# A two-layer hybrid decoder: column group 1 normed for the first tokens inside layer 0's last products, and the parameters loaded behind x's eighth block

## Chip, cores and metric

One core of one Trainium2 chip. The metric is device time in microseconds (us): the median of the runs of a kernel. Before the change three runs took 908.03, 908.29 and 909.82 us, median 908.29 us.

## What is computed

Two decoder layers on x of 256 tokens by 2048 columns (float32). Each layer makes one combined input projection, mixes its columns in three branches (a gated convolution, latent attention, an RWKV-7 scan), makes one output projection and a LayerNorm over each token's row:

```
for l in range(2):
    u = x @ w_in[l]                       # 2048 -> 6016 columns, cut into groups
    y_conv, y_mla, y_rwkv = the three branches of u
    mix = concatenate([y_conv, y_mla, y_rwkv])          # 2048 columns
    x = layer_norm(alpha * x + mix @ w_out[l], ln_g[l], ln_b[l])
```

## The kernel before

**Products in three parts.** Every float32 weight block is split into a rounded half (`hi`, a cast on ACT) and a remainder (`lo`, a subtraction on DVE); x is split in the same way. TensorE (PE) multiplies hi by hi, hi by lo and lo by hi. A weight block lands in one of five raw buffers (pool `wr`), its halves go to one of four pairs of buffers (pool `wh`); SP issues the loads in the order of `plan()`, and the next load waits for a free raw buffer, the next cast for a pair that PE has read to the end.

**Layer 0's start.** The first column group, `k`, needs all of x. `STEPS` (L215) lists the pieces in which x and the weights of `k` arrive together, each one DMA from `xT` (`load_first`, L217): pieces of one or two of the 16 blocks of 128 rows. ACT and DVE split x and the weights of each piece, and PE does 12 matmuls of 256 columns for each block. Behind the last piece (`k0 == 14`) `load_constants` (L164) makes GpSimd (POOL) copy one element of that piece and then issue the loads of `pars` (the per-channel parameters), `cs` (masks and the like), `posi` (positions) and `ones` (a matrix of ones that sums over channels). `load_params` (L248) derives eight small tables `pc` from `pars` on DVE. The group `k` is then mixed with its shifted self into `kx`: four ACT scalings, each with a DVE multiply-add behind it, that read the PSUM accumulator `u_k`. The group `a` follows on PE, in two halves, `u_a_0` and `u_a_1`.

**Accumulators.** Pool `pp` has two buffers of two PSUM banks, for `u_*` and `po_*`, so the third accumulator in a row waits until an earlier one has been read out: `u_a_1` follows `u_k` and `u_a_0`.

**The order of the instructions.** A scheduler orders each engine's instructions by data and buffers. `after(inst, earlier)` adds an order; the list `splits` holds the cast and the subtraction of each weight block in load order, so `after(v, splits[n][1])` places v behind a block's subtraction on DVE.

**From layer 0 to layer 1.** `out_proj` (L1229) makes the output projection in four groups of 512 columns, and group 3 in two halves `i` of 256, for the token halves `h` = 0 and 1. The second half of group 3 is computed for h = 0, then for h = 1. When h = 0 is complete, `root(0)` finds its mean and reciprocal deviation; `row(0)` (matmul `cwt`, cast `ct`) and `norm(0, g)` (a matmul `lw` of 512 columns, and one DVE multiply-add) finish the LayerNorm of column group g. Layer 0 does `norm(0, 0)` between the products of h = 1, at the places `AT[0] = (10, 13)` of 16, and groups 1 to 3 in `rest`, beside layer 1's first products. `add` (L1245) reads an accumulator into the residual `xr`, `keep_warm` issues 12 matmuls `pz` while PE waits for `root(1)`, and `turn` (matmuls `xt`) transposes the normed rows into x of the next layer.

Of the kernel before, what the change touches and what calls it, by code (L numbers as in the profile page):

```python
# [14 lines left out]
ALU = mybir.AluOpType  # L15
# [15 lines left out]
AT = [(10, 13), (4, 8)]  # L31
# [80 lines left out]
def hybrid_layers(ctx: ExitStack, tc: tile.TileContext, x, positions, xT, w_in, w_out, w_uq, w_ukv, par, wa_in, gb_in,  # L112
# [13 lines left out]
    gates, splits = {}, []  # L126
# [40 lines left out]
    def load_constants(x):  # L167

        last = G.tensor_copy(pars[0:1, 0, 0:1], x[0:1, 0:1])
        for to, src in ((pars, par), (cs, cst), (posi, positions[0:1, :].to_broadcast([P, S]))):  # L170
            load = nc.gpsimd.dma_start(to, src)
            after(load, last)
            last = load
        o32 = c4("ones32", (P, 2 * P))
        load = nc.gpsimd.dma_start(o32, sums)
        after(load, last)
        V.tensor_copy(ones, o32)
        loaded.append(load)

    def zeros(rows):  # L180

# [31 lines left out]
    xres = x  # L213
    xs = [pair(f"x0_{g}") for g in range(4)]

    STEPS = [(0, 1), (1, 1), (2, 2), (4, 2), (6, 2), (8, 2), (10, 2), (12, 2), (14, 2)]

    def load_first(k0, n):

        t = s8(f"first{k0}", (P, n, S + 512))  # L220
        in_turn(1, nc.sync.dma_start(t, xT[:, k0:k0 + n, :]))
        with tc.high_priority():
            to, at = xs[k0 // 4], k0 % 4
            split_in(to[:, 0, at:at + n, :], to[:, 1, at:at + n, :], t[:, :, 0:S])
        if k0 == 14:
            load_constants(t[:, 0, :])
        return t[:, :, S:].rearrange("p k (i c) -> p i k c", i=2)

# [19 lines left out]
    def load_params(l):  # L248
        pq = pars[:, l, :]
        pc = cp.tile([P, 29], F32, tag=f"pc{l}", name=f"pc{l}")  # L250
        V.tensor_scalar(pc[:, 0:13], pq[:, Q_MUR:Q_MUR + 13], -1.0, 1.0, ALU.mult, ALU.add)
        V.tensor_scalar(pc[:, 13:21], pq[:, Q_W0:Q_W0 + 8], 0.5, None, ALU.mult)
        V.tensor_scalar(pc[:, 21:25], pq[:, Q_KA:Q_KA + 4], 0.5, None, ALU.mult)
        V.tensor_scalar(pc[:, 25:29], pq[:, Q_KA:Q_KA + 4], -0.5, 1.0, ALU.mult, ALU.add)
        col = lambda j: pq[:, j:j + 1] if j < NQ else pc[:, j - NQ:j - NQ + 1]
        return dict(col=col, om=NQ - Q_MUR, hw=NQ + 13, ha=NQ + 17, hk=NQ + 21, ok=NQ + 25)

# [95 lines left out]
    def acc(name):  # L353

        return pp.tile([P, 2, 512], F32, tag="acc", name=name)
# [857 lines left out]
    def ln_rows(l):  # L1213

        t = sm.tile([P, 2, 16], F32, tag="lnp", name=f"lnp{l}", bufs=1)
        load = nc.gpsimd.dma_start(t, gbp[l])
        after(load, loaded[0])
        hi = sm.tile([P, 2, 16], F32R, tag="lnh", name=f"lnh{l}", bufs=1)
        lo = sm.tile([P, 2, 16], F32R, tag="lnl", name=f"lnl{l}", bufs=1)
        V.tensor_copy(hi, t)  # L1220
        V.tensor_tensor(lo, t, hi.bitcast(F32), ALU.subtract)
        rows = dr.tile([5, D], F32R, tag=f"lnr{l}", name=f"lnr{l}")
        for i, src in enumerate((hi[:, 0], lo[:, 0], hi[:, 0], hi[:, 1], lo[:, 1])):
            nc.gpsimd.dma_start(rows[i].rearrange("(p i) -> p i", p=P), src)
        return rows

    def out_proj(l, ms, xres, last, begin, lnr):
# [86 lines left out]

        def rest(cts):
            for g in range(1, 4):
                for h in range(2):
                    norm(h, g, cts[h])
                yield
                for h in range(2):  # L1320
                    turn(h, g)
# [20 lines left out]
        for g in range(4):  # L1342
            xr = c4(f"xr{l}_{g}", (P, 2, 512))
            after(nc.scalar.dma_start(xr, xres[0, :, g * 512:(g + 1) * 512].rearrange("(h p) c -> p h c", p=P)), begin)
            zs.append(xr)
            gt = s4(f"gb{l}_{g}", (P, 2, 512))
            after(nc.scalar.dma_start(gt, gb_in[l:l + 1, :, g * 512:(g + 1) * 512].to_broadcast([P, 2, 512])), begin)
            gs.append(gt)
            if g < 3:
                pa = acc(f"po{l}_{g}")  # L1350
                po = [pa[:, h, :] for h in range(2)]
                for k0 in ORDER:
                    ws = [weights(f"wo{l}_{g}", k0 + k) for k in (0, 2)]
                    for h in range(2):
                        part(po, h, 512, ws)
                for h in range(2):
                    add(po[h], g, 0, 512, h, g)
                continue
            po, held = [], {}
            for i in range(2):  # L1360
                pa = acc(f"po{l}_{g}_{i}")
                po.append([pa[:, h, 0:256] for h in range(2)])
                held[i] = []
                for k0 in ORDER:
                    held[i].append(weights(f"wo{l}_3_{i}", k0))
                    if not last and i == 0:
                        for h in range(2):
                            part(po[i], h, 256, held[0][-1:])
                if not last and i == 0:
                    for h in range(2):  # L1370
                        add(po[i][h], g, 0, 256, h, 3)
            cts = []

            def turn_row(h):
                ct, m = row(h)
                cts.append(ct)
                return m

            first_rows = {AT[last][0]: lambda: turn_row(0),
                          AT[last][1]: lambda: [norm(0, g_, cts[0])[0] for g_ in range(4 if last else 1)][-1]}  # L1380
            for h in range(2):
                for i in range(2):
                    if not last and i == 0:
                        continue
                    part(po[i], h, 256, held[i], first_rows if h and i else {})
                    add(po[i][h], g, i * 256, 256, h, 3 + i)
                mark.setdefault(l + 1, []).append(root(h))
            if not last:
                xs += [pair(f"x{l + 1}_{g}") for g in range(1, 4)]
            keep_warm()  # L1390
            if last:
                turn_row(1)
                part1(256, 256)
                nc.scalar.dma_start(rows(0)[:, 1], zs[0][:, 1])
                for g_ in range(1, 4):
                    norm(1, g_, cts[1], ((0, 512),) if g_ < 3 else ((0, 256), (256, 256)))
            else:
                turn(1, 0, ((0, 2),))
                t = turn(0, 0, hold=mark[l + 1][1])
                after(part0(256, 256), mark[l + 1][1])  # L1400
                mark[l + 1][1] = t
                part1(256, 256)
                nc.gpsimd.dma_start(rows(0), zs[0])
                turn(1, 0, ((2, 2),))
                turn_row(1)
                run(rest(cts))
                tick()
# [60 lines left out]
```

## Time and profile before

| | |
|---|---|
| median of 3 runs | 908.29 us |
| the profiled execution | 909.28 us |
| its span, first to last instruction | 907.5 us |
| PE busy | 893.1 us (98%) |
| DVE busy | 687.5 us (76%) |
| ACT busy | 486.1 us (54%) |
| GpSimd busy | 24.6 us (3%) |
| mean granted TensorE clock | 0.994 of full speed |
| HBM | 181 GB/s over the span |

A row of a timeline gives start and duration in us, engine, source line, operation, output and inputs, and in brackets how long the engine was idle before and what ended that. Matmuls overlap, so the distance of two starts, not a duration, is what one costs. Nearly all DVE and ACT rows carry L138, a wrapper's line, and are told apart by their tiles.

### The profile page before, as it was taken

The numbers are of one execution on the slowest core, as the hardware profiler recorded it, in microseconds if no ns is written. First come the engines' busy times: TensorE is split into PE (matmuls) and PEld (weight loads), VectorE is DVE, ScalarE is ACT, GpSimd is POOL, SyncE is SP. The second block draws the span as 40 slices with busy tenths as digits, with TensorE's granted clock in tenths as the row PEclk, the third lists the DMA queues.
The fourth block names the chain that finished last, engine by engine and source line by source line (L and its number), as shares of the span: only waits on it lengthen the run. The fifth ranks groups of instructions, "written<-read, shape, count | busy, mean of one in ns | idle before, by whom it ended". The sixth has DMA issues, their size and how long they took to land.

```text
span 907.5 us, 16003 instructions
## 1 busy us (share of the span) xinstructions
PE 893.1 (98%) x6314; PEld 786.7 (87%) x6314; DVE 687.5 (76%) x1166; ACT 486.1 (54%) x752; POOL 24.6 (3%) x47
## 2 busy tenths in 40 slices
PE   8899999999999999999999999999999999999996
PEld 8788888888889888888898888888888998988896
DVE  7677988986558987476775889799765699875665
ACT  6577546444447666544246874564444575765430
POOL 2120000000000000000020000000000000000000
PEclk9989999999999999999999999999999999999999
DMA  9755674666535654696576456646654456547832
GB/s 373 222 139 161 185 208 130 187 197 177 161 111 165 193 161 118 205 325 204 171 225 194 136 190 191 170 124 204 196 173 141 123 158 209 163 118 239 315 119 93
DMA packets 65100, 164.98 MB, mean 182 GB/s; under 512 B 15286, under 2 KB 23782, under 8 KB 65014
## 3 DMA queue, kind: packets, MB, share of 16 engines
q1 hardware_dynamic: 57264, 150.36, 54.4%
q10 hardware_dynamic: 5072, 9.57, 3.0%
q0 software_dynamic: 2688, 4.03, 1.6%
q8 instruction: 49, 0.80, 0.4%
q14 instruction: 27, 0.22, 0.1%
HBM read 158.61 MB, written 5.32 MB: 181 GB/s over the span
## 4 chain that ended last, share of the span: by engine, by line
PE 95%; DVE 2%; ACT 1%; DMA 1%; issue 0%; DVEq 0%; SPq 0%; ACTq 0%
PE po L341 7%; PE u_mg L441 7%; PE po L343 7%; PE po L342 6%; PE u_a L441 4%; PE u_cc L441 3%; PE u_cg L441 3%; PE u_mg L443 3%; PE u_v L441 3%; PE u_cb L441 3%; PE u_ch L441 3%; PE u_cq L441 3%; PE u_rg L441 3%; PE u_r L441 3%; PE u_rg L443 2%; PE u_cg L443 2%
## 5 line engine op out<-in xcount | busy, mean ns | idle before, releaser
L138 DVE TENSOR_TENSOR lo_wo<-w_wo,hi_wo 128x1024 fp32r<-128x1024 f32 x57 | 69.1, 1222 | 45.0 <-ACT hi_wo L138 44.1
L138 ACT CAST hi_wo<-w_wo 128x1024 fp32r<-128x1024 f32 x57 | 59.3, 1050 | 60.1 <-PE po L343 29.9
L441 PE MATMUL u_mg<-x,hi_mg 128*128 128x512 f32 x256 | 90.0, 396 | 0.0
L443 PE MATMUL u_mg<-x,lo_mg 128*128 128x256 f32 x256 | 71.4, 280 | 0.0
L441 PEld LDWEIGHTS u_mg<-x,hi_mg 128*128 128x128 f32 x256 | 47.9, 188 | 10.8
L441 PE MATMUL u_a<-x,hi_a 128*128 128x512 f32 x128 | 48.1, 415 | 3.1 <-DVE u_a L138 3.1
L443 PEld LDWEIGHTS u_mg<-x,lo_mg 128*128 128x128 f32 x256 | 48.3, 189 | 0.2
L341 PE MATMUL po<-hi_wo,ma 128*128 128x512 f32 (+1 forms) x128 | 46.7, 365 | 0.0
L343 PE MATMUL po<-hi_wo,ma 128*128 128x512 f32 (+1 forms) x128 | 46.5, 363 | 0.0
L342 PE MATMUL po<-lo_wo,ma 128*128 128x512 f32 (+1 forms) x128 | 46.4, 363 | 0.0
L138 ACT CAST hi_mg<-w_mg 128x1024 fp32r<-128x1024 f32 x32 | 33.6, 1049 | 23.8 <-PE u_mg L441 12.5
L441 PE MATMUL u_cc<-x,hi_cc 128*128 128x512 f32 x128 | 46.2, 403 | 0.0
L441 PE MATMUL u_cg<-x,hi_cg 128*128 128x512 f32 x128 | 46.0, 401 | 0.0
L441 PE MATMUL u_cq<-x,hi_cq 128*128 128x512 f32 x128 | 45.4, 395 | 0.0
L441 PE MATMUL u_ch<-x,hi_ch 128*128 128x512 f32 x128 | 45.3, 399 | 0.0
L441 PE MATMUL u_cb<-x,hi_cb 128*128 128x512 f32 x128 | 45.3, 399 | 0.0
L441 PE MATMUL u_v<-x,hi_v 128*128 128x512 f32 x128 | 45.3, 399 | 0.0
L441 PE MATMUL u_rg<-x,hi_rg 128*128 128x512 f32 x128 | 45.3, 394 | 0.0
L441 PE MATMUL u_r<-x,hi_r 128*128 128x512 f32 x128 | 45.1, 394 | 0.0
L138 DVE TENSOR_TENSOR lo_mg<-w_mg,hi_mg 128x1024 fp32r<-128x1024 f32 x32 | 38.8, 1222 | 6.0 <-ACT hi_mg L138 4.4
L343 PE MATMUL u_k<-x,lo_k 128*128 128x256 f32 x128 | 36.9, 288 | 0.8 <-DVE lo_k L138 0.8
L138 DVE TENSOR_TENSOR lo_rg<-w_rg,hi_rg 128x1024 fp32r<-128x1024 f32 x16 | 19.6, 1223 | 23.2 <-ACT hi_rg L138 23.2
(417 smaller groups left out, 2819.5 us busy)
## 6 DMA issues: line engine op xcount, KB each, us to landing
w_wo<-in_w_out_dram SPq DMA_DIRECT2D x64, 512.0 KB, 4.3
w_mg<-in_w_in_dram SPq DMA_DIRECT2D x32, 512.0 KB, 4.0
w_a<-in_w_in_dram SPq DMA_DIRECT2D x16, 512.0 KB, 4.5
w_r<-in_w_in_dram SPq DMA_DIRECT2D x16, 512.0 KB, 3.7
w_v<-in_w_in_dram SPq DMA_DIRECT2D x16, 512.0 KB, 3.7
w_cq<-in_w_in_dram SPq DMA_DIRECT2D x16, 512.0 KB, 3.8
w_cc<-in_w_in_dram SPq DMA_DIRECT2D x16, 512.0 KB, 4.0
w_ch<-in_w_in_dram SPq DMA_DIRECT2D x16, 512.0 KB, 3.7
```

The lines of the kernel that those rows point to most:

```text
L138: inst = call(*args, **kwargs)
L341: m = T.matmul(o, lh, rh, start=first, stop=False, skip_group_check=True)
L342: T.matmul(o, lh, rl, start=False, stop=False, skip_group_check=True)
L343: T.matmul(o, ll, rh, start=False, stop=last, skip_group_check=True)
L441: T.matmul(ps[:, b, :].rearrange("p (i t) -> p i t", i=2), hi[:, k, c], x2, start=k0 + k == 0, stop=False, skip_group_check=True)
L443: T.matmul(ps[:, b, 0:S], lo[:, k, c], x2[:, 0, :], start=False, stop=k0 + k == NKC - 1, skip_group_check=True)
```

## The change

Seven edits, in three groups. **x's start:** the piece (2, 2) is cut into (2, 1) and (3, 1), so x comes in ten pieces. **Parameters:** `load_constants` is called behind piece 6 (blocks 6 and 7), not behind the last; the cast of `ones` moves into `load_params(0)`; every instruction of `load_params` is placed behind the last subtraction of `k`, and the cast in `ln_rows` behind the first subtraction of `a`. **Layer 0's end:** h = 1 of the second half of group 3 gets an accumulator of its own, `po_3_2`; `norm(0, 1)` is done together with `norm(0, 0)` inside the products, and left out of `rest`.

```diff
@@ load_constants
         after(load, last)
-        V.tensor_copy(ones, o32)
-        loaded.append(load)
+        loaded.extend((load, o32))
...
-    STEPS = [(0, 1), (1, 1), (2, 2), (4, 2), (6, 2), (8, 2), (10, 2), (12, 2), (14, 2)]
+    STEPS = [(0, 1), (1, 1), (2, 1), (3, 1), (4, 2), (6, 2), (8, 2), (10, 2), (12, 2), (14, 2)]
...
-        if k0 == 14:
+        if k0 == 6:
             load_constants(t[:, 0, :])
@@ load_params
-        V.tensor_scalar(pc[:, 0:13], pq[:, Q_MUR:Q_MUR + 13], -1.0, 1.0, ALU.mult, ALU.add)
...
+        vs = [V.tensor_scalar(pc[:, 0:13], pq[:, Q_MUR:Q_MUR + 13], -1.0, 1.0, ALU.mult, ALU.add),
...
+        if l == 0:
+            vs.append(V.tensor_copy(ones, loaded[1]))
+        for v in vs:
+            after(v, splits[len(STEPS) - 1][1])
@@ ln_rows
-        V.tensor_copy(hi, t)
+        after(V.tensor_copy(hi, t), splits[len(STEPS)][1])
@@ out_proj
             for g in range(1, 4):
-                for h in range(2):
+                for h in range(g == 1, 2):
                     norm(h, g, cts[h])
...
-                po.append([pa[:, h, 0:256] for h in range(2)])
+                pb = pa if last or i == 0 else acc(f"po{l}_{g}_2")
+                po.append([pa[:, 0, 0:256], pb[:, 1, 0:256]])
...
-                          AT[last][1]: lambda: [norm(0, g_, cts[0])[0] for g_ in range(4 if last else 1)][-1]}
+                          AT[last][1]: lambda: [norm(0, g_, cts[0])[0] for g_ in range(4 if last else 2)][-1]}
```

DVE behind x's last piece, before (`lo_k_14` is the last subtraction of group `k`, `lo_a_0_0` to `lo_a_1_12` are those of `a`):

```order
L138 TENSOR_TENSOR lo_k_14_297<-first_285,hi_k_14_296 128x1024
L138 TENSOR_TENSOR lo_a_0_0_327<-w_a_0_0_324,hi_a_0_0_326 128x1024
L138 TENSOR_TENSOR lo_a_0_4_357<-w_a_0_4_354,hi_a_0_4_356 128x1024
L138 TENSOR_TENSOR lo_a_0_8_400<-w_a_0_8_397,hi_a_0_8_399 128x1024
L138 TENSOR_TENSOR lo_a_0_12_428<-w_a_0_12_425,hi_a_0_12_427 128x1024
L138 TENSOR_SCALAR pc_384<-pars 128x13
```

and DVE at the same place now:

```order
L138 TENSOR_TENSOR lo_k_14_304<-first_299,hi_k_14_303 128x1024
L138 TENSOR_SCALAR pc_391<-pars 128x13
L138 TENSOR_SCALAR pc_391<-pars 128x8
L138 TENSOR_SCALAR pc_391<-pars 128x4 x2
L138 CAST ones<-ones_185 128x256
L138 TENSOR_SCALAR pc_5098<-pars 128x13
L138 TENSOR_SCALAR pc_5098<-pars 128x8
L138 TENSOR_SCALAR pc_5098<-pars 128x4 x2
L138 TENSOR_TENSOR lo_a_0_0_334<-w_a_0_0_331,hi_a_0_0_333 128x1024
L138 CAST lnh_2898<-lnp_2896 128x32
```

The eight tables of both layers and the cast of `ones` have moved in front of the four subtractions of `u_a_0`, and so has the wait for the loads of `pars` and `ones`.

DVE around the last `kx` of layer 0 (`u_a` here is the read-out of the accumulator `u_a_0`), before:

```order
L138 SCALAR_TENSOR_TENSOR kx_389<-u_k_88,pars,kx_389 128x255
L138 TENSOR_SCALAR ang<-ang 128x256
L138 SCALAR_TENSOR_TENSOR nn<-ang 128x256
L138 TENSOR_TENSOR lo_a_1_12_552<-w_a_1_12_549,hi_a_1_12_551 128x1024
L138 TENSOR_SCALAR nn<-nn 128x256
L138 TENSOR_TENSOR u_a_0_507<-u_a_0_507,u_a_0_396 128x512
L138 SCALAR_TENSOR_TENSOR kx_389<-u_k_88,pars,kx_389 128x255
```

and now:

```order
L138 TENSOR_TENSOR lo_a_1_4_496<-w_a_1_4_493,hi_a_1_4_495 128x1024
L138 SCALAR_TENSOR_TENSOR ang<-nn,ang 128x256
L138 SCALAR_TENSOR_TENSOR kx_397<-u_k_88,pars,kx_397 128x255
L138 SCALAR_TENSOR_TENSOR ang<-nn,ang 128x256
L138 CAST lnh_7590<-lnp_7588 128x32
L138 SCALAR_TENSOR_TENSOR ang<-nn,ang 128x256
L138 TENSOR_TENSOR lnl_7591<-lnp_7588,lnh_7590 128x32
L138 TENSOR_TENSOR lo_a_1_8_530<-w_a_1_8_527,hi_a_1_8_529 128x1024
```

The fourth `kx`, which stood behind `lo_a_1_12` and the read-out of `u_a_0`, stands behind `lo_a_1_4`; and the first matmul of `u_a_1`, which waited for the read-out of `u_a_0`, now waits for that `kx`.

PE at layer 1's first products, before (`xt` are the transposes, `u_k` layer 1's first accumulator, `lw_0_1` the matmul of `norm(0, 1)`):

```order
L1307 MATMUL xt_1_0_2_4776<-cs,xr_0_4001 128x128 x2
L1286 MATMUL cwt_1_4781<-cs,cw_3993 5x128
L341 MATMUL u_k_4792<-x_0_3999,hi_k_0_4608 128x256
L1295 MATMUL lw_0_1_0_4785<-gr_3997,ct_0_4709 128x512
L342 MATMUL u_k_4792<-x_0_3999,hi_k_0_4608 128x256
L343 MATMUL u_k_4792<-x_0_3999,lo_k_0_4609 128x256
L341 MATMUL u_k_4792<-x_0_3999,hi_k_0_4608 128x256
```

and PE inside layer 0's last products now (`po_3_2` is the accumulator of h = 1):

```order
L345 MATMUL po_3_2_4604<-wlwo_3_1_8_4610,ma_1_3990 128x256
L346 MATMUL po_3_2_4604<-wlwo_3_1_8_4610,ma_1_3990 128x256
L1298 MATMUL lw_0_0_0_4729<-gr_4005,ct_0_4718 128x512
L1298 MATMUL lw_0_1_0_4732<-gr_4005,ct_0_4718 128x512
L344 MATMUL po_3_2_4604<-wlwo_3_1_8_4610,ma_1_3990 128x256
L345 MATMUL po_3_2_4604<-wlwo_3_1_8_4610,ma_1_3990 128x256
L346 MATMUL po_3_2_4604<-wlwo_3_1_8_4610,ma_1_3990 128x256
L344 MATMUL po_3_2_4604<-wlwo_3_1_8_4610,ma_1_3990 128x256
```

The matmul of `norm(0, 1)` has come from between layer 1's first two products to behind that of `norm(0, 0)`, with nine products of h = 1 left behind it.

## Rows read from the trace of the kernel before

**Rows 1.** From the page: the busy time of the engines, and the chain of work that ended last, by engine.

```profile
PE 893.1 (98%) x6314; PEld 786.7 (87%) x6314; DVE 687.5 (76%) x1166; ACT 486.1 (54%) x752; POOL 24.6 (3%) x47
...
PE 95%; DVE 2%; ACT 1%; DMA 1%; issue 0%; DVEq 0%; SPq 0%; ACTq 0%
```

**Rows 2.** PE's waits over the span: what waited for what, us in total, times, longest.

```profile
PE u_a L441 <- DVE u_a L138: 3.1, 1, 3.1
PE u_k L343 <- DVE lo_k L138: 0.8, 1, 0.8
PE po L341 <- DVE xr L138: 0.5, 1, 0.5
```

**Rows 3.** Timeline of PE, 5 to 13 us: the matmul ahead of the gap, a hi one of the first group's third block of x, and the lo one behind it, which needs that block's subtracted weights.

```profile
8.89 0.28 PE L342 MATMUL u_k<-x,hi_k 128*128 128x256 f32 x1
9.93 0.39 PE L343 MATMUL u_k<-x,lo_k 128*128 128x256 f32 x1 [0.76 <-DVE lo_k L138]
```

**Rows 4.** Timelines of ACT, and behind the dots of DVE, in the same stretch: x's second, third and fourth block as they are cast (the third and fourth in one), and the subtraction of the weights of the next piece, (4, 2).

```profile
4.19 0.40 ACT L138 CAST x<-first 128x256 fp32r<-128x256 f32 x1 [2.16 <-DMA first<-in_xT_dram]
5.15 0.41 ACT L138 CAST x<-first 128x256 fp32r<-128x256 f32 x1
7.04 0.62 ACT L138 CAST x<-first 128x512 fp32r<-128x512 f32 x1 [0.97 <-DMA first<-in_xT_dram]
...
10.53 1.22 DVE L138 TENSOR_TENSOR lo_k<-first,hi_k 128x1024 fp32r<-128x1024 f32 x1
```

**Rows 5.** Timeline of PE, 26 to 52 us: the first subtracted block of `u_a_0`, its last matmul, the first of `u_a_1`, and where the pace changes.

```profile
30.17 0.28 PE L443 MATMUL u_a<-x,lo_a 128*128 128x256 f32 x1
...
41.13 0.28 PE L443 MATMUL u_a<-x,lo_a 128*128 128x256 f32 x1
44.49 0.79 PE L441 MATMUL u_a<-x,hi_a 128*128 128x512 f32 x1 [3.08 <-DVE u_a L138]
...
50.41 0.46 PE L441 MATMUL u_a<-x,hi_a 128*128 128x512 f32 x1
50.83 0.40 PE L441 MATMUL u_a<-x,hi_a 128*128 128x512 f32 x1
51.18 0.40 PE L441 MATMUL u_a<-x,hi_a 128*128 128x512 f32 x1
```

**Rows 6.** Busy time in two stretches of 5 us: PE, PEld, DVE, ACT, POOL (x instructions), then the granted clock, the DMA share, GB/s.

```profile
10.00:15.00 5.00, 5.00 (x42) 5.00 (x43) 4.84 (x6) 4.05 (x6) 1.08 (x2) 1.00 1.00 415
45.00:50.00 5.00, 5.00 (x17) 4.24 (x16) 1.36 (x2) 3.52 (x8) 4.69 (x9) 0.50 0.64 134
```

**Rows 7.** Timeline of DVE, 30 to 45 us: the eight tables `pc` (both layers'), the subtraction of `lo_a_1_4`, the read-out of `u_a_0` and the fourth `kx`.

```profile
32.47 0.68 DVE L138 TENSOR_SCALAR pc<-pars 128x13 f32<-128x13 f32 x8
...
36.81 1.23 DVE L138 TENSOR_TENSOR lo_a<-w_a,hi_a 128x1024 fp32r<-128x1024 f32 x1 [0.18 <-ACT hi_a L138]
...
43.75 0.68 DVE L138 TENSOR_TENSOR u_a<-u_a,u_a 128x512 f32<-128x512 f32 x1
44.35 0.48 DVE L138 SCALAR_TENSOR_TENSOR kx<-u_k,pars,kx 128x255 f32<-128x255 f32 x1
```

**Rows 8.** Timeline of GpSimd, 18 to 23 us, and behind the last dots, from the issues of DMAs in 0 to 60 us, the load of `ones` (size, median us from issue to landing).

```profile
18.40 0.93 POOL L169 COPY pars<-first 1x1 f32<-1x1 f32 x1 [3.56 <-DMA first<-in_xT_dram]
19.64 0.73 POOL L171 DMA_DIRECT2D pars<-in_par_dram  x1 [0.31 <-POOL pars L169]
...
21.43 0.54 POOL L175 DMA_DIRECT2D ones<-in_sums_dram  x1
...
ones<-in_sums_dram POOLq DMA_DIRECT2D x1, 128.0 KB, 6.3
```

**Rows 9.** DMA queues in two stretches: packets, MB, share of 16 engines. The row above the dots is the only queue of 22 to 23 us, the one below is the first of 24 to 25 us; q1 is SP's queue, q0 GpSimd's.

```profile
q1 hardware_dynamic: 120, 0.43, 107.1%
...
q0 software_dynamic: 95, 0.34, 91.3%
```

**Rows 10.** Timelines of PE, and behind the last dots of DVE, 441 to 462 us: the turn from h = 0 to h = 1, the first transposes, two `lw` in a row and the matmul behind them; then the multiply-add of `norm(0, 0)`, and the `add` of h = 1.

```profile
441.51 0.28 PE L343 MATMUL po<-wlwo,ma 128*128 128x256 f32 x1
442.30 0.38 PE L341 MATMUL po<-hi_wo,mc 128*128 128x256 f32 x1 [0.51 <-DVE xr L138]
...
451.85 1.38 PE L1307 MATMUL xt<-cs,xr 128*128 128x128 f32 x8 [0.42 <-PE pz L1339]
...
460.95 0.72 PE L1295 MATMUL lw<-gr,ct 5*128 5x512 f32 x2
461.60 0.39 PE L343 MATMUL u_k<-x,lo_k 128*128 128x256 f32 x1
...
447.78 0.75 DVE L138 SCALAR_TENSOR_TENSOR xr<-xr,rstd,lw 128x512 f32<-128x512 f32 x1
449.05 0.42 DVE L138 SCALAR_TENSOR_TENSOR xr<-xr,po 128x256 f32<-128x256 f32 x1 [0.53 <-PE po L343]
```

**Rows 11.** Busy time in stretches of 10 us, columns as in rows 6.

```profile
60.00:70.00 10.00, 10.00 (x59) 8.84 (x58) 9.66 (x12) 7.70 (x12) 0.00 (x0) 1.00 0.55 156
70.00:80.00 10.00, 10.00 (x64) 8.98 (x63) 7.14 (x9) 6.42 (x12) 0.00 (x0) 1.00 0.63 210
80.00:90.00 10.00, 10.00 (x59) 8.68 (x58) 6.10 (x7) 8.27 (x13) 0.00 (x0) 1.00 0.37 107
...
110.00:120.00 10.00, 10.00 (x76) 8.77 (x75) 10.00 (x16) 3.04 (x5) 0.00 (x0) 1.00 0.70 217
```

More of the change, by code (lines that the diff above doesn't have):

```diff
@@ L250, in load_params @@
         pc = cp.tile([P, 29], F32, tag=f"pc{l}", name=f"pc{l}")
-        V.tensor_scalar(pc[:, 0:13], pq[:, Q_MUR:Q_MUR + 13], -1.0, 1.0, ALU.mult, ALU.add)
-        V.tensor_scalar(pc[:, 13:21], pq[:, Q_W0:Q_W0 + 8], 0.5, None, ALU.mult)
-        V.tensor_scalar(pc[:, 21:25], pq[:, Q_KA:Q_KA + 4], 0.5, None, ALU.mult)
-        V.tensor_scalar(pc[:, 25:29], pq[:, Q_KA:Q_KA + 4], -0.5, 1.0, ALU.mult, ALU.add)
+        vs = [V.tensor_scalar(pc[:, 0:13], pq[:, Q_MUR:Q_MUR + 13], -1.0, 1.0, ALU.mult, ALU.add),
+              V.tensor_scalar(pc[:, 13:21], pq[:, Q_W0:Q_W0 + 8], 0.5, None, ALU.mult),
+              V.tensor_scalar(pc[:, 21:25], pq[:, Q_KA:Q_KA + 4], 0.5, None, ALU.mult),
+              V.tensor_scalar(pc[:, 25:29], pq[:, Q_KA:Q_KA + 4], -0.5, 1.0, ALU.mult, ALU.add)]
+        if l == 0:
+            vs.append(V.tensor_copy(ones, loaded[1]))
+        for v in vs:
+            after(v, splits[len(STEPS) - 1][1])
         col = lambda j: pq[:, j:j + 1] if j < NQ else pc[:, j - NQ:j - NQ + 1]
```

## Prediction

> **What bounds the kernel now.** The share of busy time comes first: PE is busy for 98% of the span, and 95% of the chain that ended last is PE's own work [rows 1]. So a change is worth what it takes out of PE's idle or slowed time, and work moved on DVE or GpSimd counts only where PE waits for it. The table of PE's waits is therefore the next view; three of its lines lie where the diff does: `u_a` behind DVE's `u_a` (3.1), the lo matmul of `u_k` (0.8), and `po` behind `xr` (0.5) [rows 2]. The timelines give the place and the whole gap of each [rows 3, 5, 10]. The stretches of time add what the waits can't tell: in 45 to 50 us PE is fully busy, at a granted clock of 0.50 [rows 6].
>
> All sums stand against the profiled execution's 909.28 us (span 907.5); it is 0.99 above the median of 908.29, so I take the differences and subtract them from the median too. About 0.2%, 1.8 us, is what a measurement here can tell from no change.
>
> **1. Cutting the piece (2, 2).** The lo matmul that needs the third block's weights starts at 9.93; the hi matmul ahead of it started at 8.89 and matmuls of 256 columns follow each other by 0.12, so PE loses 9.93 − 9.01 = 0.92 us [rows 3]. Block 1 alone was cast 5.15 − 4.19 = 0.96 behind block 0, the pair behind it 7.04 − 5.15 = 1.89 later [rows 4]: with one block in a transfer, block 2 comes 0.9 earlier, and its cast and subtraction are shorter by half or start sooner. Two singles cost 2 × 0.96 − 1.89 = 0.03 more than one pair, so later pieces keep their time. The next demand is the piece (4, 2): its subtraction ends at 10.53 + 1.22 = 11.75 [rows 4]; PE, without the gap, has 22 matmuls left of the blocks 2 and 3 from 9.01 on and two hi ones ahead of the next lo, and asks at 9.01 + 24 × 0.12 = 11.89. That fits without slack, so the bounds are 0.5 and 0.92; I take **0.92**, as the rows meet. Each pair of blocks after that is 24 × 0.12 = 2.88 us of PE against 1.89 of transfer, so PE's slack grows by 1.0 a piece.
>
> The Trainium skill, "DMA: Bandwidth & Descriptors", section "Rules for kernel authors", says to coalesce many small transfers into one large one, and its section "Anatomy of one DMA" puts some 2.0 us of fixed cost on each that GpSimd issues. On this queue the rows show 0.03; by the page the sum would be about 1.9 smaller.
>
> **2. The parameters.** GpSimd's copy waits for a piece of x. It now waits for the piece of blocks 6 and 7, which by 1.89 a pair is there at 7.04 + 2 × 1.89 = 10.8, not 18.40. `pars` follows 1.24 and `ones` 3.03 behind the copy [rows 8], so they are issued at 12.05 and 13.85. GpSimd's queue then carries 1,336 columns of 128 rows (`pars`, `cs`, `posi`, `ones`), 684 KB or 1.7 us at the rate of x (384 KB a block in 0.96), beside x's pieces from (8, 2) on; PE's slack there is 2 us and more. What is moved in front of `lo_a_0_0` is small: eight tables 0.68 and a cast of about 0.3 [rows 7]. But DVE, which is in order, now waits there for the landing T of `ones`. Early bound: 13.85 + 6.3 = 20.2. Late bound: 21.43 + 6.3 = 27.7, as before [rows 8], for at 22 to 23 us only SP's queue moved packets, although `pars` and `ones` had been issued, and at 24 to 25 GpSimd's had 91% of the engines [rows 9]: the constants got through when SP's backlog was gone, which an earlier issue need not change. Behind T stand the cast, the second layer's half of the tables and the 1.22 of the subtraction, about 1.7 in all. PE asks for `lo_a_0_0` at 30.17 − 0.92 = 29.25 [rows 5], so the stall is T − 27.55: nothing by the early bound, 0.15 by the late. I take **−0.15**, since rows 9 show the backlog.
>
> The Trainium skill, same page, section "SWDGE vs HWDGE vs iDMA", says that each DMA engine round-robins between the queues that the two kinds feed. By that T would be near the early bound, and the sum 0.15 larger; rows 9 do not look like turns.
>
> Behind the waiting DVE stand five subtractions, and behind these the raw buffers, so SP's loads stop after the fifth. They resume with each subtraction, and 512 KB at x's rate is 1.3 us, against 2.8 of PE's products per block of `a` (eight pairs of 0.35, rows 5): no cost. `lnp` follows `ones` by one issue, 0.5, and stands behind `lo_a_0_0`: covered by the same 2.8.
>
> **3. `u_a_1`.** Its first matmul would follow 41.13 by 0.12; it starts at 44.49, 3.24 late [rows 5], because the read-out of `u_a_0`, 43.75 to 44.43, had to free a buffer [rows 7]. Now it uses the buffer of `u_k`, free with the fourth `kx`. That stands behind `lo_a_1_4`, which ended at 36.81 + 1.23 = 38.04 at the pace of PE's reads; 0.77 less for parts 1 and 2, plus some 0.9 of work between, gives 38.2. Counted as DVE work from 29.4 on (five subtractions of 1.14, four `kx` of 0.40, small ones of 1.5) it is 38.2 too; with a late load up to 39.3. PE asks at 41.25 − 0.77 = 40.5: 1.2 to 2.3 to spare, so the gap goes: **3.24**. What is late next? The second layer's `lnh` waits in front of `lo_a_1_8` for a load and writes of GpSimd, but PE wants that block only two blocks on, at 40.5 + 2 × 2.8 = 46.
>
> With the gap goes the slow clock behind it: from 44.49 to 50.41 nine pairs of matmuls took 5.92, where a pair takes 51.18 − 50.83 = 0.35 afterwards [rows 5]; nine are 3.15, so **2.8** comes back. The gap of 0.92 at 9 us did not lower the clock: 1.00 in 10 to 15 [rows 6]. Together 6.0.
>
> **4. The turn to h = 1 and `norm(0, 1)`.** With an accumulator of its own h = 1 starts 0.12 behind 441.51, not at 442.30: 0.67 [rows 10]. The second `lw` inside the products costs its 512 columns at 0.12 for 256, 0.24; two in a row held PE for 461.60 − 460.95 = 0.65, which is no more than 0.33 each. So the `add` of h = 1 (449.05), and with it the path to the transposes (451.85), comes 0.43 sooner; DVE's second multiply-add (0.75, as at 447.78) fits in the idle time in front of that `add` [rows 10]. The place the second `lw` leaves, between layer 1's first products, covered a wait for DVE and gives nothing back. Bounds −0.3 (DVE late by 0.75) and 0.67; I take **0.43**.
>
> **Sum:** 0.92 − 0.15 + 6.0 + 0.43 = 7.2, so 902.1 on the profiled execution and **901.1** against the median.
>
> **Rivals.** (a) Part of the wait at `u_a_1` stays: the fourth `kx` comes over 2.3 later than worked out, 1 us is idle, and the clock falls as before: 901.1 + 1 + 2.8 = 904.9. For: DVE's queue from 29.4 on is nearly gapless, and each cast ahead may wait. Against: two counts that agree. (b) The change doesn't do what it says, and `u_a_1` still waits for something as late as the read-out: only 0.92 − 0.15 + 0.43 = 1.2 is left, 907.1, within 0.2%. (c) DVE takes back half: near 110 us it is busy for 10.00 of 10 [rows 11], and would set the pace there. Against: it has 0.34 + 2.86 + 3.90 = 7.1 us free in 60 to 90, enough to arrive earlier too. Half is 3.6: 904.7. (d) The extra transfer has a fixed cost of its own, as long as a pair's transfer (1.89): (4, 2) and what follows come so much later, PE waits, and it is 903.0; against it stand the 0.03 of rows 4. The rule of the Trainium skill named in part 1 is this one. (e) **Slower:** the constants hold DVE. All of `a` then shifts by T − 27.55, and the clock falls behind the stall (2.8 more); against the 7.35 of the other gains, slower by over 1.8 from T = 33.9 on. At T = 36 it is 8.45 + 2.8 − 7.35 = 3.9, 912.2. Against: SP's loads stop at five buffers, so nothing keeps the constants out beyond 27.7.
>
> **How the numbers follow.** Forecast 0.72, (a) 0.11, (b) 0.06, (c) 0.06, (d) 0.02, (e) 0.03. All but (b) and (e) are faster: 0.91; same 0.06; slower 0.03. High end: 905.0 takes in (a) and (c). Low end: with 0.67 for part 4 and no wait for `ones`, 900.7, less 0.9, half the distance between the lowest and highest of the three runs: 899.8.
>
> **What would show it.** Right: no wait at the lo matmul of `u_k` near 9 us; `ones` cast by 28 and the first lo matmul of `u_a_0` at 29.3 to 29.5; no wait at `u_a_1` and a clock of 1.00 throughout 40 to 50; no `po` behind `xr`; the transposes 7.2 earlier, and all that follows by as much. Wrong: `u_a` still in PE's waits with a clock of 0.50 behind it; a PE wait at 11.9; DVE's full stretch at its old time; or the cast of `ones` past 33.

## The result, and the profile after

The changed kernel takes 903.04 us (median of 4 runs, 902.87 to 903.10) against 909.06 us (4 runs, 908.03 to 910.03): ratio 0.9934, 95% interval 0.9916 to 0.9951, 6.0 us faster. Forecast were 901.1 us, 7.2 less. Beside the experiments the kernel before ran far more often, with medians of 908.25 to 908.58 over 11 to 21 runs; against the last of these the changed kernel's 903.26 is 5.3 less. So 5.3 to 6.0 us is the gain, and most of the uncertainty is the kernel before: its runs lie between 906.7 and 911.7, those of the changed kernel between 902.87 and 903.92.

The profiled execution of the changed kernel took 902.87 us, span 901.1. Its page, against [rows 1]: PE is busy 3.3 us less; 2.69 of it lies in the stage behind `u_a_1`, where the products at half clock are gone.

```profile
PE 889.8 (99%) x6314; PEld 784.4 (87%) x6314; DVE 687.9 (76%) x1168; ACT 485.9 (54%) x754; POOL 25.0 (3%) x47
```

PE's waits (what waited for what, us in total, times, longest), against [rows 2]:

```profile
PE pzero L243 <- DVE zeror L138: 1.9, 1, 1.9
PE cwt L1289 <- DVE cw L138: 1.0, 1, 1.0
PE u_k L346 <- DVE lo_k L138: 0.7, 1, 0.7
PE lw L1298 <- DVE ct L138: 0.6, 1, 0.6
PE pq L344 <- ACT vt L138: 0.5, 2, 0.2
PE u_k L345 <- DVE x L138: 0.4, 1, 0.4
PE xt L1310 <- DVE xr L138: 0.4, 1, 0.4
```

`u_a` behind DVE and `po` behind `xr` are gone. The wait of the lo matmul of `u_k` is still there with 0.7, which was forecast to go.

To see where the 6.4 us between the two executions lie, cut each span at matmuls that both kernels have, and subtract their starts (stages of PE, in us):

| stage on PE | before | after | difference | forecast |
|---|---|---|---|---|
| start to the first lo matmul of `u_a_0` | 30.17 | 29.96 | −0.21 | −0.77 |
| to the first matmul of `u_a_1` | 14.32 | 11.08 | −3.24 | −3.24 |
| to the first of `u_r` | 14.90 | 12.21 | −2.69 | −2.8 |
| to the first of `u_v` | 24.17 | 24.45 | +0.28 | 0 |
| to the first transpose of layer 1's x | 368.29 | 367.74 | −0.55 | −0.43 |
| to the last four matmuls, a group `lw` | 449.22 | 449.11 | −0.11 | 0 |

In the eight profiles that have the whole parameter part of the change, the three stages from `u_a_0` to `u_v` repeat to 0.01 us; the stage of the transposes repeats to 0.05 among the kernels that share its code, and the last to 0.2. So such a table tells tenths of a us that medians can't. The first stage does not repeat: 29.91 to 30.47 for the changed start.

**`u_a_1`.** Timeline of PE, against [rows 5]: the last matmul of `u_a_0`, the first of `u_a_1`, and one nine pairs on; then the stretches that answer to [rows 6].

```profile
40.92 0.28 PE L446 MATMUL u_a<-x,lo_a 128*128 128x256 f32 x1
41.04 0.40 PE L444 MATMUL u_a<-x,hi_a 128*128 128x512 f32 x1
...
44.22 0.40 PE L444 MATMUL u_a<-x,hi_a 128*128 128x512 f32 x1
```

```profile
40.00:45.00 5.00, 5.00 (x30) 4.34 (x29) 4.45 (x7) 4.94 (x8) 4.49 (x8) 1.00 0.97 228
45.00:50.00 5.00, 5.00 (x29) 4.27 (x28) 3.66 (x5) 3.49 (x4) 0.00 (x0) 1.00 0.90 255
```

The two accumulators follow each other by 0.12, nine pairs (a matmul of 512 columns and one of 256) take 44.22 − 41.04 = 3.18, and the granted clock is 1.00 where it was 0.50.

DVE's timeline, against [rows 7]: the cast of `ones`, the fourth `kx`, the read-out of `u_a_0`.

```profile
24.05 0.29 DVE L138 CAST ones<-ones 128x256 fp32r<-128x256 f32 x1
...
38.02 0.48 DVE L138 SCALAR_TENSOR_TENSOR kx<-u_k,pars,kx 128x255 f32<-128x255 f32 x1
...
43.80 0.68 DVE L138 TENSOR_TENSOR u_a<-u_a,u_a 128x512 f32<-128x512 f32 x1
```

The fourth `kx` ends at 38.5 (38.2 was worked out) and PE asks at 41.04; the read-out ends when it did before, and nobody waits for it. `ones` is cast at 24.05, almost 6 us before the products need `lo_a_0_0`, with no wait ahead of it.

**The turn.** PE's timeline, against [rows 10]: last matmul of h = 0 and first of h = 1, the two `lw` and the matmul behind them, the first transpose.

```profile
435.67 0.28 PE L346 MATMUL po<-wlwo,ma 128*128 128x256 f32 x1
435.79 0.28 PE L344 MATMUL po<-hi_wo,mc 128*128 128x256 f32 x1
...
440.65 0.72 PE L1298 MATMUL lw<-gr,ct 5*128 5x512 f32 x2
441.30 0.39 PE L344 MATMUL po<-wlwo,ma 128*128 128x256 f32 x1
...
445.44 1.43 PE L1310 MATMUL xt<-cs,xr 128*128 128x128 f32 x8 [0.38 <-DVE xr L138]
```

435.79 follows 435.67 by 0.12, and the two `lw` hold PE for 0.65, as two did before.

**The start.** PE's timeline around x's pieces, against [rows 3]; then ACT's casts of the blocks 1, 2, 3 and of the piece (4, 2), and DVE's subtraction of that piece, against [rows 4].

```profile
8.83 0.28 PE L346 MATMUL u_k<-x,lo_k 128*128 128x256 f32 x1
...
11.59 0.28 PE L345 MATMUL u_k<-x,hi_k 128*128 128x256 f32 x1
12.60 0.38 PE L346 MATMUL u_k<-x,lo_k 128*128 128x256 f32 x1 [0.73 <-DVE lo_k L138]
```

```profile
5.07 0.41 ACT L138 CAST x<-first 128x256 fp32r<-128x256 f32 x1
...
6.02 0.41 ACT L138 CAST x<-first 128x256 fp32r<-128x256 f32 x1
...
7.71 0.41 ACT L138 CAST x<-first 128x256 fp32r<-128x256 f32 x1 [0.76 <-DMA first<-in_xT_dram]
...
9.71 0.62 ACT L138 CAST x<-first 128x512 fp32r<-128x512 f32 x1 [1.08 <-DMA first<-in_xT_dram]
...
11.32 1.23 DVE L138 TENSOR_TENSOR lo_k<-first,hi_k 128x1024 fp32r<-128x1024 f32 x1 [0.26 <-ACT hi_k L138]
```

Block 2 comes 0.95 behind block 1, and its lo matmul starts at 8.83 without a wait. But block 3 comes 1.69 behind block 2, and the piece (4, 2) at 9.71, 0.8 later than 7.04 + 1.89 of [rows 4]. Its subtraction ends at 12.55, and PE waits there, from 11.71 to 12.60. The wait has moved by one piece.

**The constants.** GpSimd's copy and first load, the landing time of `pars`, and the two queues in 16 to 20 us (packets, MB, share of 16 engines), against [rows 8, 9].

```profile
11.59 0.99 POOL L169 COPY pars<-first 1x1 f32<-1x1 f32 x1 [11.14 <-DMA first<-in_xT_dram]
12.89 0.73 POOL L171 DMA_DIRECT2D pars<-in_par_dram  x1 [0.31 <-POOL pars L169]
...
pars<-in_par_dram POOLq DMA_DIRECT2D x1, 91.0 KB, 5.7
...
q1 hardware_dynamic: 219, 1.06, 65.2%
q0 software_dynamic: 150, 0.51, 36.2%
```

GpSimd's queue (q0) moves a third of the bytes while SP's (q1) still carries x and the weights of `a`. The loads didn't wait for SP's backlog: the first packet of GpSimd's queue came 3.9 us behind the issue of `pars` in both executions, at 16.75 here and at 23.50 behind 19.64 in the kernel before, and 2.9 to 4.0 behind it in all twelve profiles.

### The profile page after: what moved, and what is told of

It reads as the page before. It is cut to its first block, busy times and chain, and to the rows that moved or that the text cites. A ratio compares the mean times of both kernels' runs of the same rounds, so it can differ in the third digit from the quotient of the medians.

```text
span 901.1 us, 16013 instructions
## 1 busy us (share of the span) xinstructions
PE 889.8 (99%) x6314; PEld 784.4 (87%) x6314; DVE 687.9 (76%) x1168; ACT 485.9 (54%) x754; POOL 25.0 (3%) x47
## 4 chain that ended last, share of the span: by engine, by line
PE 96%; DVE 2%; ACT 1%; issue 0%; DVEq 0%; ACTq 0%
PE po L344 7%; PE u_mg L444 7%; PE po L346 7%; PE po L345 7%; PE u_cc L444 3%; PE u_cg L444 3%; PE u_mg L446 3%; PE u_cb L444 3%; PE u_ch L444 3%; PE u_v L444 3%; PE u_a L444 3%; PE u_cq L444 3%; PE u_r L444 3%; PE u_rg L444 3%; PE u_rg L446 2%; PE u_cg L446 2%
## 5 line engine op out<-in xcount | busy, mean ns | idle before, releaser
L444 PE MATMUL u_a<-x,hi_a 128*128 128x512 f32 x128 | 45.5, 398 | 0.0
```

Source lines behind the costliest of these rows:

```text
L444: T.matmul(ps[:, b, :].rearrange("p (i t) -> p i t", i=2), hi[:, k, c], x2, start=k0 + k == 0, stop=False, skip_group_check=True)
```

## The experiments

Ten runs, one of them the changed kernel once more. What a text calls a stage is one of the table above. The diffs are against the changed kernel, but for the early load alone and the filled gap, which are edits of the kernel before.

### The changed kernel without the cut

```diff
-    STEPS = [(0, 1), (1, 1), (2, 1), (3, 1), (4, 2), ...
+    STEPS = [(0, 1), (1, 1), (2, 2), (4, 2), ...
```

> The changed kernel with x's third and fourth block in one transfer again. Theory: the cut only moved PE's wait from the third piece to the piece (4, 2), since the single transfer of block 3 came 0.7 us late; it is worth some 0.2 us, so this runs at 903.2 against 903.0 of the changed kernel, with the wait of 0.8 at the lo matmul of u_k back at 9 us. Rival: the cut is worth the 0.9 of the forecast and the missing gain was lost elsewhere: 903.9.

Measured: 903.09 us (902.91 to 903.80, 5 runs), against 903.04 and 903.26 with the cut. The first stage took 30.16. The theory's time came out, though not by its wait of 0.8: this execution lost only 0.2 there. Two rows of PE's start in it, and two a little later:

```profile
7.16 0.41 PE L345 MATMUL u_k<-x,hi_k 128*128 128x256 f32 x1
7.37 0.41 PE L346 MATMUL u_k<-x,lo_k 128*128 128x256 f32 x1
...
7.91 0.28 PE L346 MATMUL u_k<-x,lo_k 128*128 128x256 f32 x1
8.03 0.28 PE L344 MATMUL u_k<-x,hi_k 128*128 128x256 f32 x1
```

Until 7.59 matmuls of 256 columns follow each other by 0.21, then by 0.12: in this execution PE kept its slower pace for longer (in the profile of [rows 3] the faster one began at 6.24), and met the third piece's subtraction at its own pace. The granted clock reads 1.00 in this stretch of both profiles, so what makes the slow start is not shown. It lasted to 6.1 to 6.3 in eight of the twelve profiles and to 7.6 to 8.1 in four, with and without the cut. One of the four is that of the changed kernel without its part at the end of layer 0, further down: it has the cut, no wait at (4, 2), and a first stage of 29.91. In these executions the pace of PE, and not the landing of x, sets the end of the stage, and a cut has little to win.

The transfer rate shows what the cut does. Stretch 5 to 6 us (columns as in [rows 6]; the last is GB/s), the changed kernel and then the one without the cut:

```profile
5.00:6.00 1.00, 1.00 (x4) 0.68 (x4) 0.92 (x2) 0.97 (x3) 0.00 (x0) 1.00 1.03 261
```

```profile
5.00:6.00 1.00, 1.00 (x4) 0.58 (x3) 0.91 (x3) 1.00 (x3) 0.00 (x0) 1.00 0.99 412
```

In all four profiles with the four single blocks in a row (changed kernel twice, and two below) the rate in this stretch is 200 to 283 GB/s; in the seven with at most two in a row, all on SP's queue, it is 387 to 442. By 10 us the four have moved 2.73 to 2.92 MB and the seven 3.13 to 3.22. Against the mean of the seven the loss is 0.2 to 0.4 MB, which is 0.5 to 1.0 us at 420 GB/s, and it falls on block 3 and what follows: the piece (4, 2) is cast at 9.58 to 10.21 in the four, and at 8.91 to 9.72 in the five that load blocks 2 and 3 as one piece. The two ranges overlap, since pairs scatter too, so the loss of rate is shown and the lateness of one execution is not all its work. SP was not late with the issues (the first seven transfers, ten blocks, were issued by 4.0 us); why the engines move less there is not shown.

### One transfer for blocks 2 and 3, split in two behind it

```diff
+        if k0 == 3:
+            t = turn["two"][:, 1:2, :]
+        else:
+            m = 2 if k0 == 2 else n
+            t = s8(f"first{k0}", (P, m, S + 512))
+            in_turn(1, nc.sync.dma_start(t, xT[:, k0:k0 + m, :]))
...
```

> The changed kernel with blocks 2 and 3 in one transfer, but cast and subtracted block by block as the cut has it. Theory: it is the extra transfer that brought block 3 late; with one transfer the casts of the pair start at about 7.0, block 2's subtraction is done by 8.8 and the piece (4, 2) is at 8.9 as in the kernel before, so neither wait is left, and the time is 0.7 us under the changed kernel: 902.3. Rival: not the landing but the order of casts and subtractions of four small pieces makes the wait at (4, 2): it stays, 903.0 or more.

Measured: 902.79 us (901.92 to 903.52, 5 runs). The rate stays at 390 to 430 GB/s from 3 us on, so the dip goes with the transfers, not with the casts behind them; but the pair landed at 8.14 in this execution (7.03 to 7.85 in others with a pair there), and two waits of 0.2 remained, first stage 30.28. Time 0.3 to 0.5 under the changed kernel, inside both spreads: not decided.

### The cut at another piece

```diff
-    STEPS = [(0, 1), (1, 1), (2, 1), (3, 1), (4, 2), ...
+    STEPS = [(0, 1), (1, 1), (2, 2), (4, 1), (5, 1), (6, 2), ...
```

> The changed kernel with the piece (4, 2) cut into (4, 1) and (5, 1) in place of (2, 2). Theory A: every transfer beyond the ninth costs some 0.7 us on SP's queue whichever piece is cut: the pieces behind block 5 land 0.7 later than with pairs, PE has slack there, and the wait of 0.8 at the third piece is back: 903.2. Theory B: four single-block transfers in a row are what the queue can't feed; here there are two, a pair and two, all land at 0.96 and 1.89 steps, and the time is the same 903.2: the casts of x tell A from B. Rival: the cut is worth 0.9 wherever it is: 903.9 or 902.9.

Measured: 903.79 us (903.04 to 903.91, 5 runs); first stage 30.83, with waits of 0.47 and 0.76 for the third piece. x was cast at 7.70, 9.18, 10.01, 11.53 and 13.41, and the rate stayed between 393 and 452 GB/s. With pairs alone behind a third piece cast at 7.67 (the parameter part alone, below) the casts that follow block 5 stand at 11.44 and 13.31, so the extra transfer cost them 0.1 and not 0.7. So B: it is single blocks in a row that cost, not an extra transfer as such. The median is the 903.9 of the rival, but its reason, a cut worth 0.9, falls with the kernel that has no cut and runs at 903.09.

### Block 3 on ACT's queue

```diff
+        if k0 == 3:
+            nc.scalar.dma_start(t, xT[:, k0:k0 + n, :])
+        else:
+            in_turn(1, nc.sync.dma_start(t, xT[:, k0:k0 + n, :]))
```

> The changed kernel with the single transfer of block 3 issued on ACT's queue, the others on SP's. Theory: what delays block 3 lies in SP's queue (its transfers are fed one behind the other), so on a queue of its own it comes beside the others: block 3 is cast by 7.0 or sooner, the others a little later, and PE's wait at (4, 2) shrinks below 0.4: 902.5. Rival: the DMA engines themselves are what is full; moving the issue changes nothing, 903.0, or makes the first pieces late by the 384 KB that come in between: up to 904.

Measured: 907.89 us (906.41 to 908.84, 11 runs), 4.6 to 4.9 slower than the changed kernel. ACT's rows, the issue and the cast of that block:

```profile
4.15 0.38 ACTq L221 DMA_DIRECT2D first<-in_xT_dram  x1
...
12.44 0.40 ACT L138 CAST x<-first 128x256 fp32r<-128x256 f32 x1 [5.46 <-DMA first<-in_xT_dram]
```

ACT put the issue behind its first wait, at 4.15, 2 us later than SP's; the transfer then shared the engines with four pairs and landed 8.3 us later. So the run doesn't tell whether SP's queue was the limit. The rate dipped here too, to 292 GB/s in 5 to 6 us, with three single blocks in a row on SP's queue and the fourth on ACT's; whether three are enough, or ACT's transfer did it, is not separated. What the run shows is the price of a late piece: PE waited 2.40, and the granted clock fell behind that wait (PE's first matmul after it, and the stretch 15 to 20, columns as in [rows 6]).

```profile
13.41 0.39 PE L347 MATMUL u_k<-x,hi_k 128*128 128x256 f32 x1 [2.40 <-ACT hi_k L138]
...
15.00:20.00 5.00, 5.00 (x32) 5.00 (x32) 5.00 (x6) 4.88 (x8) 1.19 (x3) 0.70 1.00 379
```

The first stage ends 4.5 later than in the changed kernel: 3.9 at the end of the waits, 1.5 more by the half clock, less the 0.9 that the changed kernel loses at (4, 2).

### The changed kernel with the constants late

```diff
-        if k0 == 6:
+        if k0 == 14:
             load_constants(t[:, 0, :])
```

> The changed kernel with the parameters loaded behind x's last piece again; the ordering edits in load_params stay, and the scheduler then places the fourth kx behind the read-out of u_a_0, as it stood before the change. Theory: the early load gives the whole 6 us by letting the fourth kx stand behind lo_a_1_4; without it u_a_1 waits about 3.2 us again and the granted clock falls to 0.50 behind it: 909.0. Rival: that placement is not what PE waited for, and the ordering edits carry the gain: 903.0.

Measured: 907.38 us (906.14 to 908.49, 11 runs), 4.1 to 4.3 slower than the changed kernel. DVE's read-out of `u_a_0` with the fourth `kx` behind it, the first matmul of `u_a_1` on PE, and the stretch 45 to 50:

```profile
43.84 0.68 DVE L138 TENSOR_TENSOR u_a<-u_a,u_a 128x512 f32<-128x512 f32 x1
44.43 0.48 DVE L138 SCALAR_TENSOR_TENSOR kx<-u_k,pars,kx 128x255 f32<-128x255 f32 x1
```

```profile
44.57 0.51 PE L444 MATMUL u_a<-x,hi_a 128*128 128x512 f32 x1 [3.08 <-DVE u_a L138]
```

```profile
45.00:50.00 5.00, 5.00 (x22) 4.30 (x21) 1.42 (x2) 4.45 (x9) 4.65 (x8) 0.66 0.57 124
```

The stage up to `u_a_1` is 14.32 again, to the hundredth as before. The stage behind it is 13.75, not 14.90: the half clock came and went, but its spell covered fewer products (0.66 in 45 to 50 against 0.50 in [rows 6]; by the us, the granted clock is 0.50 from 44 to 50 in the kernel before, and here 1.00 in 44 to 45 and 0.50 from 46 to 49). So the early load makes the gain. That it does so by the place of the fourth `kx` is read from these rows; no run moved that instruction alone. What the clock takes behind one and the same wait differs from execution to execution by over 1 us. The two kernels with this wait and the half clock scatter over 2.4 (11 runs) and 5.0 us (51 runs), the changed kernel over 1.1 (10 runs).

### The early load alone, in the kernel before

```diff
-        if k0 == 14:
+        if k0 == 6:
             load_constants(t[:, 0, :])
```

> The kernel before with one edit: the parameters are loaded behind the piece of blocks 6 and 7. The scheduler then puts the tables pc in front of the subtraction of x's fifth pair (block 8) and the cast of ones in front of that of block 12, and the fourth kx behind lo_a_1_4. Theory: the early load alone brings the 6 us at u_a_1; pars lands at about 18 and holds DVE there, so PE waits some 1.7 us for lo_k of block 8; together about 4.3 us under the kernel before, 904.5, and 2.8 more if the clock falls behind that wait. Rival: constants that share the engines with x land earlier than 17 and there is no wait: 902.9.

Measured: 905.16 us (904.87 to 906.19, 5 runs). The stage to `u_a_1` is 11.08 and the next one 12.10: the whole gain is there. But DVE stood still for `pars` with x's subtractions behind it:

```profile
19.07 0.47 DVE L138 TENSOR_SCALAR pc<-pars 128x13 f32<-128x13 f32 x5 [4.64 <-DMA pars<-in_par_dram]
```

PE's waits in the start, and its stretch 10 to 15:

```profile
9.47 0.39 PE L341 MATMUL u_k<-x,hi_k 128*128 128x256 f32 x1 [0.70 <-ACT hi_k L138]
...
10.73 0.39 PE L343 MATMUL u_k<-x,lo_k 128*128 128x256 f32 x1 [0.76 <-DVE lo_k L138]
...
21.53 0.39 PE L343 MATMUL u_k<-x,lo_k 128*128 128x256 f32 x1 [0.42 <-DVE lo_k L138]
```

```profile
10.00:15.00 5.00, 4.27 (x23) 4.27 (x24) 4.33 (x5) 4.37 (x6) 3.06 (x5) 0.67 1.02 422
```

The wait for `pars` itself cost PE only 0.42, since PE had already lost time: two waits for a late third piece, and a clock of 0.67 behind them. The first stage is 33.13, 3 us longer than in the profile before; this execution, at 906.19, lies 1.0 above the median of its kernel. The ordering edits of the change (all tables behind the last subtraction of `k`) can save only the part that is DVE's wait; with them, in the next kernel, the median is 1.2 lower.

### The parameter part alone

```diff
-    STEPS = [(0, 1), (1, 1), (2, 1), (3, 1), (4, 2), ...
+    STEPS = [(0, 1), (1, 1), (2, 2), (4, 2), ...
...
-                pb = pa if last or i == 0 else acc(f"po{l}_{g}_2")
+                pb = pa
```

(and `norm(0, 1)` back in `rest`)

> The kernel before with the parameter part alone (early load, all tables behind the last subtraction of k). Theory: u_a_1 starts without a wait and at full clock, as in the changed kernel, and the constants hold nobody; 0.6 to 1.2 for the turn and 0.1 for the cut are missing: 903.8 to 904.4. Rival: without the cut or the turn part the scheduler or the loads bring back a part of the wait at u_a: 905 or more.

Measured: 903.95 us (903.71 to 905.03, 6 runs) against 908.58 of the kernel before and 903.26 of the changed kernel: 4.6 of the 5.3 us. Stages 11.08 and 12.21.

### The changed kernel without its part at the end of layer 0

```diff
-                for h in range(g == 1, 2):
+                for h in range(2):
...
-                pb = pa if last or i == 0 else acc(f"po{l}_{g}_2")
+                pb = pa
...
-                          AT[last][1]: lambda: [norm(0, g_, cts[0])[0] for g_ in range(4 if last else 2)][-1]}
+                          AT[last][1]: lambda: [norm(0, g_, cts[0])[0] for g_ in range(4 if last else 1)][-1]}
```

> The changed kernel without its part at the end of layer 0 (h = 1 in the accumulator of h = 0, norm(0, 1) in the rest). Theory: that part is worth the 0.67 of the wait less 0.24 for the second lw, 0.4 to 0.5 us: 903.5, with PE's wait of 0.5 at po behind xr back. Rival: the second lw's place between layer 1's products was a cost of its own, and the part is worth 0.7 or more: 903.8; or DVE's second multiply-add delays the add and it is worth nothing: 903.0.

Measured: 904.29 us (903.62 to 904.45, 5 runs). The wait is back:

```profile
PE po L344 <- DVE xr L138: 0.5, 1, 0.5
```

The stage from `u_v` to the transposes is 368.33, against 367.74 with it: 0.59. The last stage is 449.24 against 449.11, a difference that kernels with the same code there also show. So by the stages this part is worth 0.6 to 0.7, a little over the theory. The medians say more: 1.0 to 1.25 against the changed kernel, and 0.9 between the parameter part alone (903.95) and the kernel without the cut (903.09), which differ by this part. The profiled execution, at 903.62, lies 0.7 under the median of its kernel, so it can't show where the rest lies; the rival's 0.7 or more is not excluded.

### The gap filled with products

```diff
+            if (l, name, i) == (0, "a", 1):
+                pz = pm.tile([P, 512], F32, tag="m", name="pzgap")
+                for _ in range(13):
+                    mark["gap"] = T.matmul(pz, xs[0][:, 0, 0, 0:P], xs[0][:, 0, 0:2, :], start=True, stop=True)
+                    after(mark["gap"], mark["ua"])
...
+                        if (l, name, i) == (0, "a", 1):
+                            after(m0, mark["gap"])
```

> The kernel before with 13 products of 512 columns, whose result nobody reads, between the last product of u_a_0 and the first of u_a_1. They fill about 3.0 of the 3.24 us that PE waits there. Theory: the half clock behind that wait comes of PE's idling, so it does not fall, and nine pairs of products run at 0.35 in place of 0.64: 2.8 us less, about 906. Rival: the slow pace has another cause (DVE or the loads): no change, 908.8.

Measured: 908.15 us (907.18 to 908.71, 11 runs), no change. But the stage is as the theory has it:

```profile
41.69 3.12 PE L437 MATMUL pzgap<-x 128*128 128x512 f32 x13
44.93 0.50 PE L446 MATMUL u_a<-x,hi_a 128*128 128x512 f32 x1
```

```profile
45.00:50.00 5.00, 5.00 (x29) 4.39 (x30) 1.68 (x4) 4.71 (x9) 4.30 (x8) 1.00 0.65 128
```

`u_a_1` begins as late as before (14.32), the clock stays at 1.00, and the stage behind it takes 12.14 in place of 14.90. What it gained was lost elsewhere: 0.44 in the start, and 1.3 in the stage from `u_v` to the transposes (369.58), where the small products `pg` stand in another order among those of `cq`. So the idle gap is the cause of the half clock; the total of this kernel says nothing on it.

### The changed kernel again

> The changed kernel once more, beside the kernels that leave out parts of it. Theory: its start ends by the landing of x, which differs by some tenths from one execution to the next, so its median is that of the kernel without the cut, 903.1 within 0.4. Rival: the cut is worth 0.7 or more and the first four runs were slow ones: 902.4 or less.

Measured: 903.26 us (903.05 to 903.92, 6 runs); first stage 30.47, with a wait of 0.8 at the piece (4, 2). The median is the theory's, and the rival falls. The kernel without its part at the end of layer 0 and the parameter part alone differ by the cut only: 904.29 with it, 903.95 without. So no median shows a gain by the cut.

## Why the prediction was nearly right

**Part 3, `u_a_1`: right** in place, size and cause. 3.24 and 2.69 of 3.24 and 2.8; the fourth `kx` done at 38.5, where 38.2 was worked out; rivals (a), (b) and (c) fell. (The late bound of 39.3 for that `kx` has no sum in the text; nothing came near it.) The runs with the constants late and with the gap filled show both halves apart. One thing was missed: I took one profiled spell of half clock for a constant. In another execution it cost 1.15 less, and the kernel before has a median nearer 908.4 than the 909.28 that the sum was made on.

**Part 1, the cut: mis-sized.** The step that failed is "Two singles cost 0.03 more than one pair, so later pieces keep their time". It rests on two rows that compare a first single with the pair behind it [rows 4], and there are no three singles in a row in the trace of before. Four in a row lost 0.5 to 1.0 us of transfer, and since (4, 2) had no slack, as the text itself worked out, PE waited there, 0.89 to 0.92 in three of the four profiles: the wait at 11.9 that the prediction named as a sign of being wrong. A second thing was missed: the 0.92 was taken from one execution with a quick start, and where PE starts slowly there is little to win. First stages with the cut were 29.91 to 30.47, with the pair 30.16 to 30.80, and the medians 903.04 and 903.26 against 903.09: the cut is worth 0.2 or 0.3 at best, not 0.92, and no median shows that it is worth anything. Rival (d) had the mechanism, at a quarter to a half of its price; that its 903.0 is the measured time is luck. The Trainium skill's rule ("DMA: Bandwidth & Descriptors", "Rules for kernel authors": coalesce many small transfers) points the same way. The 2.0 us of fixed cost that its section "Anatomy of one DMA" gives for a transfer issued by GpSimd is two to four times what was lost here on SP's queue.

**Part 2, the constants: near in size, wrong in reasoning.** 0.15 of stall was taken, and there was none. From one microsecond with SP's packets alone [rows 9] I read that the constants wait for SP's backlog. In the changed kernel they moved 0.51 MB in 16 to 20 us beside SP's 1.06. The first packet came 3.9 us behind the issue in both kernels, with SP's queue running dry at that point in the one and still loaded in the other, so the silence at 22 to 23 us needs no backlog; `pars` took 5.7 from issue to landing, against 5.4 before. What sharing the engines costs shows in `ones`, 8.7 against 6.3: issued at 14.68, it landed at 23.4, between the two bounds and 4 us ahead of the 27.55 from which PE would have stalled. The Trainium skill (same page, "SWDGE vs HWDGE vs iDMA") has each DMA engine round-robin between the queues; the rows, with 36% and 65% of the engines' time for the two queues in 16 to 20 us, agree with it in that both moved at once. The price fell on x: its last piece was cast at 21.02 in place of some 18.4, within PE's slack.

**Part 4, the turn: right, a little low:** 0.55 from the two profiles, 0.59 from the kernel without it, where 0.43 was taken (by medians 0.9 to 1.25, of which no profile shows the rest). The wait of 0.67 went in full; what the second `lw` costs was put too high. That the place it leaves gives nothing back holds within 0.1, the scatter of the last stage.

**Not foreseen:** the stage of `u_r` became 0.28 longer, with the same products, no wait, and the clock at 1.00. The first 40 of its 64 pairs of products take 0.3533 each on average in the changed kernel and 0.3467 in the kernel before, which is 0.27; the last pairs run alike. Within the stage the pace changes only where other products (`pw`, `pa`) stand between the pairs. The stage is short with the wait at `u_a_1` (before) and without it (early load alone, 24.17), and it is 24.25 with the constants late and 24.29 with the gap filled, so the wait isn't the cause; it stays open.

In all: forecast −7.24, measured by stages −6.52. Cut +0.71 (with 0.15 back for the constants the first stage is off by 0.56), `u_r` +0.28, clock +0.11, turn −0.12, last stage −0.11. That is 0.7 of the 1.9 by which the median missed the forecast of 901.1. Nearly all the rest is the step that took the differences, worked out on an execution 0.99 above its median, from the median: the profiled execution of the changed kernel lies 0.17 under its own.

## What to carry to other kernels

Read what order the scheduler will make of an earlier load, not only when the data land: here the rows say that the load mattered because it let one short instruction stand ahead of another on DVE, and an order set by hand kept the early work off the critical inputs. A gap on PE is priced with the clock behind it, as a range, since the same gap cost 1.5 to 2.7 us more. And a price for one more transfer must come from rows with as many in a row.

## What the runs showed of the hardware

- With four single transfers of 384 KB in a row on SP's queue the rate in 5 to 6 us was 200 to 283 GB/s (four profiles of four), with at most two in a row 387 to 442 (seven of seven); with three in a row and a fourth on ACT's queue 292.
- From GpSimd's issue of `pars` to the first packet of its queue 2.9 to 4.0 us passed in twelve profiles, 3.9 both where SP's queue ran dry at that point (before) and where it was still loaded (changed kernel).
- Around a PE wait of 3.1 us the granted clock fell to 0.50 of full speed, its lower level (1.2 GHz of 2.4), in both kernels that have it, and behind 2.4 too (0.50 from 15 to 18 us). Behind two waits of 0.70 and 0.76 it also fell (0.67 on average in 10 to 15 us, early load alone); behind 0.47 and 0.76 (the cut at another piece) and behind the one of 0.76 in the kernel before it stayed at 1.00. With the gap of 3.1 filled by products it stayed at 1.00.
- Products of 512 and 256 columns in turn ran at one of two mean paces in the stage of `u_r`, 0.3467 or 0.3533 us a pair, both at a granted clock of 1.00; the cause is open.
